# Strassen's scheme for the down products of the FFN, with sums of the hidden rows kept in DRAM

## The chip, the cores and the metric

The kernel runs on one core of a Trainium2 chip. The metric is the device time of one execution in microseconds (us); lower is better. The engines are PE (TensorE: matmuls, with its weight loads), DVE (VectorE), ACT (ScalarE), POOL (GpSimd) and SP (which issues the DMAs). Each engine works through its own instructions strictly in the order in which they were written into its queue, and waits at the first one that isn't ready.

## The reference

A step of a decoder with two layers, in fp32: 1024 prompt tokens and 64 sample tokens, width 1024. Layer 0 mixes tokens with a gated MLP, layer 1 with sliding-window attention; both have the same feed-forward network (FFN), whose hidden width is 2816:

```python
def swiglu_ffn(h, w_gate, w_up, w_down):
    return (jax.nn.silu(h @ w_gate) * (h @ w_up)) @ w_down
...
        x = x + rms_norm(out, sg_norm_post[layer] if layer < N_A_LAYERS else sw_norm_post[layer - N_A_LAYERS])
        h = rms_norm(x, f_norm_pre[layer])
        x = x + rms_norm(swiglu_ffn(h, f_w_gate[layer], f_w_up[layer], f_w_down[layer]), f_norm_post[layer])
```

The change concerns the last product, `@ w_down` (2816 to 1024 columns), in both layers.

## The kernel before

An fp32 product is made of three passes over fp32r operands. Each operand is split into a high part (ACT copies it, L275 or L510) and a low part (DVE subtracts, L276 or L511); PE then multiplies high by high, low by high and high by low. So every product costs three matmuls, and every operand one ACT copy and one DVE subtraction before PE may use it.

The hidden width is 22 feature tiles of 128, in 11 pairs. Gate and up products run pair by pair by Strassen's scheme over halves of the tokens (x: blocks 0 to 3, y: blocks 4 to 7 of 128 tokens). Each hidden tile that is finished is stored to DRAM (`store`, 256 KB each, four for a pair).

The down product comes after the last pair, in `ffn`. The 22 tiles are taken in six groups of 3, 3, 4, 4, 4 and 4. For a group, `fetch` loads the hidden tiles (all tokens, 544 KB each) and splits them, and the queue `W` delivers the split rows of `w_down`. `down(b, h, ...)` then computes block `b` (8 prompt blocks, one of samples) for one half of the columns into one PSUM bank: 3 matmuls (L1235) for each tile of the group. At its end the bank is added to the block's accumulator, a row of 1024 columns in SBUF, by DVE (L1240; ACT copies, L1238, in the first group). One block follows the other, so banks close one at a time. The next group's `fetch` is written behind the first block.

In the last group each block is finished as soon as its two banks are in (`Exit.second`): ACT squares and sums the row (L1040), DVE and POOL form the inverse root (L862, L863), DVE scales (L1042) and adds the residual row (L1043). Layer 1 then writes the result out (L1045). Layer 0 stores it (L1048), squares it again (L1049), scales it with an ACT copy (L1051), and `turn` transposes three blocks at a time on PE (L1062) for the attention of layer 1. The samples carry their two parts in two halves of 128 rows, which a small product folds (L1245, copied by L1246). The residual row of the next block is loaded while one block is finished.

The program is written in this order, but what sets the order on each engine is a scheduler that places all instructions ahead of time; on the chip the order is fixed.

Of the kernel before, what the change touches and what calls it, by code (L numbers as in the profile page):

```python
# [9 lines left out]
F32 = mybir.dt.float32  # L10
# [4 lines left out]
ALU = mybir.AluOpType  # L15
# [16 lines left out]
GROUPS = [3, 3, 4, 4, 4, 4]  # L32
HN = 512
ORDER = [0, 1, 2, 3, 8, 4, 5, 6, 7]
HD = 64
# [66 lines left out]
def trunk_kernel(ctx, tc, a):  # L102
# [317 lines left out]
    def add_ffn(layer):  # L420
        for q in range(NF):
            W.add_quad(a[("f_w_gate", "f_w_up")[q % 2]][layer], q // 2 * 2, (layer, q))
        for f in range(NF):
            W.add(a["f_w_down"][layer][f * P:(f + 1) * P, :], 1, D)
# [600 lines left out]
    class Exit:  # L1025
# [32 lines left out]
        def turn(self, c, k):  # L1058
# [5 lines left out]
            if c == 0:  # L1064
                self.x.append(act_pair())
# [15 lines left out]
    def ffn(layer, ent, last):  # L1081

        hid = [mk(dpool, [P, T], F32, f"hid{layer}_{f}") for f in range(NF)]
# [8 lines left out]
        def store(q, i, c):  # L1092
            nc.sync.dma_start(hid[q // 2 * 2 + i][:, c * HN:(c + 1) * HN], region(q, i, c))
# [11 lines left out]

        def need(name):
            flow.drain(lambda: ent.gate[name].is_open)

        def p1(q):
            need("x1")  # L1110
            if q % 2 == 0:
                rows[q // 2] = [special([P, D], "rows", bufs=2) for _ in range(2)]
# [3 lines left out]
            s["keep"] = region(q, 0, 1) if q % 2 == 0 else tmp()  # L1116
            nc.scalar.activation(s["keep"], s["a"], AF.Copy)  # L1117

        def p2(q):
            need("x2")  # L1120
            s = st[q]
            part(s["a"], unit(q, "b2"), 0, ent, "x2", False)
            r = region(q, 0, 0)
# [21 lines left out]
        def turned(q, cp):  # L1145
# [12 lines left out]
            else:  # L1158
# [3 lines left out]
                for i in range(2):  # L1162
                    nc.sync.dma_start(hid[q // 2 * 2 + i][:, SEQ:], r[:, i, :])
# [27 lines left out]
        def p3(q):  # L1191
# [4 lines left out]
            take(q, 0, 1, s["c"], s["u2"])  # L1196

# [4 lines left out]
        for fn, q in steps:  # L1202
            fn(q)
            flow.run()


        W.cap = 6
        W.prepare()
        acc = [act_tile()[:, :D] for _ in range(NB + 1)]
        parts = deque()  # L1210

        def fetch(g):
            f = sum(GROUPS[:g])
            new = []
            hs = act_tile(F32R)[:, :GROUPS[g] * P].rearrange("p (f s t) -> p f s t", s=2, t=NS)
            for i in range(GROUPS[g]):
                h, l = act_pair()
                nc.sync.dma_start(l.bitcast(F32), hid[f + i])
                split(hs[:, i, 0, :], hs[:, i, 1, :], l[:, SEQ:].bitcast(F32))
                split(h[:, :SEQ], l[:, :SEQ], l[:, :SEQ].bitcast(F32))  # L1220
                new.append((h, l))
            parts.append((new, hs.rearrange("p f s t -> p f (s t)")))

        def down(b, h, us, xs, hs, gi):
            ps = bank()
            o, n = slice(h * HN, (h + 1) * HN), len(us)
            for i, u in enumerate(us):
                wh, wl = u.hi[:, 0, o], u.lo[:, 0, o]
                if b < NB:
                    xh, xl = (t[:, b * P:(b + 1) * P] for t in xs[i])  # L1230
                    todo = [(xh, wh), (xl, wh), (xh, wl)]
                else:
                    todo = [(hs[:, i, :], wh), (hs[:, i, :], wl)]
                for j, (x, w) in enumerate(todo):
                    nc.tensor.matmul(ps, x, w, start=i == j == 0, stop=i == n - 1 and j == len(todo) - 1)  # L1235
            flow.pe(3 * n * HN / 2.4)
            if gi == 0:
                nc.scalar.activation(acc[b][:, o], ps, AF.Copy)  # L1238
            else:
                nc.vector.tensor_tensor(acc[b][:, o], ps, acc[b][:, o], op=ALU.add)  # L1240

        def folded():
            for h in range(2):
                ps = bank()
                nc.tensor.matmul(ps[:NS, :], fold, acc[NB][:, h * HN:(h + 1) * HN], start=True, stop=True)  # L1245
                nc.scalar.activation(z8[:NS, h * HN:(h + 1) * HN], ps[:NS, :], AF.Copy)  # L1246
            flow.pe(1800)
            ext.second(NB, z8)

        fetch(0)  # L1250
        for gi, gn in enumerate(GROUPS):
            xs, hs = parts.popleft()
            us = [W.get() for _ in range(gn)]
            order = list(range(NB + 1))
            final = gi == len(GROUPS) - 1
            if final:
                W.cap = 5
                ext = Exit(lambda b: ent.out[:tokens(b), b, :], ("f_norm_post", layer), last)
                order = [NB] + order[:-1] if last else order[:6] + [NB] + order[6:-1]
                ext.fetch(order[0])  # L1260
                z8 = act_tile()[:, :D]
            for j, b in enumerate(order):
                if final and j < NB:
                    ext.fetch(order[j + 1])
                for h in range(2):
                    down(b, h, us, xs, hs, gi)
                    if j == NB and h:
                        for u in us:
                            W.done(u)
                    flow.run()  # L1270
                if j == 0 and not final:
                    fetch(gi + 1)
# [404 lines left out]
```

## Time and profile before

| what | value |
|---|---|
| median of 3 runs | 2274.45 us (2274.03 to 2278.57) |
| profiled execution, its own time | 2275.59 us |
| its span | 2273.9 us |
| PE busy | 2202.6 us, 97% of the span |
| DVE busy | 1283.2 us, 56% |
| ACT busy | 810.4 us, 36% |
| DMA | 194.69 MB, mean 86 GB/s |
| down products of layer 0 | from 855.9 to about 1126.9 us |
| down products of layer 1 | from about 2004 to 2264.6 us |

The time of the profiled execution stands 1.7 us over its span. "x" in a row is a count of instructions. `PEclk` is the clock that PE was granted, 1.00 being full speed. In rows of the timeline the first two columns are the start and the length in us, and "[2.92 <-ACT act L510]" says that the engine sat idle for 2.92 us before the row, until ACT's line 510 released it. Tiles carry the names `bank` and `aux` (PSUM), `act` (SBUF operands, accumulators), `rows` and `raw` (what was loaded), `tok` (one number for a token).

### The profile page before, as it was taken

The numbers are of one execution on the slowest core, as the hardware profiler recorded it, in microseconds if no ns is written. First come the engines' busy times: TensorE is split into PE (matmuls) and PEld (weight loads), VectorE is DVE, ScalarE is ACT, GpSimd is POOL, SyncE is SP. The second block draws the span as 40 slices with busy tenths as digits, with TensorE's granted clock in tenths as the row PEclk, the third lists the DMA queues.
The fourth block names the chain that finished last, engine by engine and source line by source line (L and its number), as shares of the span: only waits on it lengthen the run. The fifth ranks groups of instructions, "written<-read, shape, count | busy, mean of one in ns | idle before, by whom it ended". The sixth has DMA issues, their size and how long they took to land.

```text
span 2273.9 us, 29115 instructions
## 1 busy us (share of the span) xinstructions
PE 2202.6 (97%) x11392; PEld 1864.3 (82%) x11392; DVE 1283.2 (56%) x2081; ACT 810.4 (36%) x1647; POOL 182.3 (8%) x222
## 2 busy tenths in 40 slices
PE   8999996999999999999999999969999999999998
PEld 7999875888888887888898877758888888878886
DVE  5465448655655653545757774477565565535446
ACT  5234424322322333211566762234232332342112
POOL 2322210000000000000213320110000000000000
PEclk9999998999999999999999998979999999999999
DMA  4211332122222234223441111221222221343224
GB/s 147 57 38 38 96 106 86 61 71 90 76 64 89 76 106 138 91 77 104 136 118 43 47 60 57 98 88 64 74 85 63 80 86 62 97 143 109 77 86 143
DMA packets 138975, 194.69 MB, mean 86 GB/s; under 512 B 22051, under 2 KB 101653, under 8 KB 138838
## 3 DMA queue, kind: packets, MB, share of 16 engines
q1 hardware_dynamic: 138838, 192.84, 26.8%
q8 instruction: 89, 1.46, 0.3%
q14 instruction: 48, 0.39, 0.1%
HBM read 143.88 MB, written 43.32 MB: 82 GB/s over the span
## 4 chain that ended last, share of the span: by engine, by line
PE 73%; DVE 5%; DMA 3%; ACT 2%; issue 1%; SPq 0%; POOL 0%; POOLq 0%; ACTq 0%; DVEq 0%
PE bank L1235 22%; PE bank L1076 11%; PE bank L1077 11%; PE bank L1078 11%; PE bank L1138 2%; PE bank L1137 2%; PE bank L873 2%; PE bank L874 1%; PE bank L505 1%; PE bank L504 1%; PE bank L506 1%; PE bank L875 1%; DVE act L276 1%; DMA act<-hid 1%; DMA raw<-in_f_w_down 1%
## 5 line engine op out<-in xcount | busy, mean ns | idle before, releaser
L1235 PE MATMUL bank<-act,act 128*128 128x512 f32 x2288 | 526.5, 392 | 5.9 <-ACT act L510 5.3
L1076 PE MATMUL bank<-act,act 128*128 128x512 f32 x1232 | 487.0, 396 | 31.0 <-ACT rows L1117 17.9
L276 DVE TENSOR_TENSOR act<-raw,act 128x1024 fp32r<-128x1024 f32 x261 | 317.5, 1223 | 352.0 <-PE bank L1077 188.3
L1235 PEld LDWEIGHTS bank<-act,act 128*128 128x128 f32 x2288 | 430.0, 189 | 100.7 <-ACT act L510 7.8
L275 ACT ACTIVATE act<-raw 128x1024 fp32r<-128x1024 f32 x261 | 275.2, 1059 | 597.7 <-PE bank L1235 203.9
L1077 PE MATMUL bank<-act,act 128*128 128x512 f32 x1232 | 485.2, 394 | 0.0
L1078 PE MATMUL bank<-act,act 128*128 128x512 f32 x1232 | 478.6, 391 | 1.2 <-DVE act L276 1.2
L1076 PEld LDWEIGHTS bank<-act,act 128*128 128x128 f32 x1232 | 232.8, 189 | 78.4 <-ACT rows L1117 18.3
L1078 PEld LDWEIGHTS bank<-act,act 128*128 128x128 f32 x1232 | 232.6, 189 | 51.0 <-DVE act L276 2.7
L1077 PEld LDWEIGHTS bank<-act,act 128*128 128x128 f32 x1232 | 233.2, 189 | 43.1
L1240 DVE TENSOR_TENSOR act<-bank,act 128x512 f32<-128x512 f32 x180 | 123.5, 688 | 150.9 <-PE bank L1235 150.7
L504 PE MATMUL bank<-act,act 128*128 128x384 f32 (+1 forms) x624 | 205.8, 332 | 2.0 <-DVE act L636 1.4
L506 PE MATMUL bank<-act,act 128*128 128x384 f32 (+1 forms) x624 | 206.8, 332 | 0.4 <-DVE act L276 0.4
L505 PE MATMUL bank<-act,act 128*128 128x384 f32 (+1 forms) x624 | 206.4, 331 | 0.0
L863 POOL TENSOR_TENSOR tok<-tok,expo 128x1 f32<-128x1 f32 (+1 forms) x63 | 54.5, 866 | 1719.3 <-DVE tok L862 1719.3
L504 PEld LDWEIGHTS bank<-act,act 128*128 128x128 f32 x624 | 117.7, 189 | 4.0 <-DVE act L636 1.6
L506 PEld LDWEIGHTS bank<-act,act 128*128 128x128 f32 x624 | 117.6, 189 | 1.9 <-issue 1.2
L505 PEld LDWEIGHTS bank<-act,act 128*128 128x128 f32 x624 | 117.8, 189 | 1.0 <-issue 0.7
L873 PE MATMUL bank<-act,act 128*128 128x512 f32 (+1 forms) x288 | 114.9, 402 | 0.6 <-DVE tok L899 0.6
L874 PE MATMUL bank<-act,act 128*128 128x512 f32 (+1 forms) x288 | 113.7, 395 | 0.0
L875 PE MATMUL bank<-act,act 128*128 128x512 f32 (+1 forms) x288 | 111.8, 393 | 0.0
L511 DVE TENSOR_TENSOR act<-act,act 128x64 fp32r<-128x64 f32 (+3 forms) x114 | 71.9, 657 | 49.9 <-ACT act L510 49.3
(231 smaller groups left out, 2628.0 us busy)
## 6 DMA issues: line engine op xcount, KB each, us to landing
act<-hid SPq DMA_DIRECT2D x44, 544.0 KB
raw<-in_f_w_gate SPq DMA_DIRECT2D x44, 512.0 KB
raw<-in_f_w_up SPq DMA_DIRECT2D x44, 512.0 KB
hid<-rows SPq DMA_DIRECT2D x88, 256.0 KB
raw<-in_f_w_down SPq DMA_DIRECT2D x44, 512.0 KB
stream<-act SPq DMA_DIRECT2D x24, 512.0 KB
rows<-stream SPq DMA_DIRECT2D x24, 512.0 KB
raw<-in_sg_w_in SPq DMA_DIRECT2D x16, 512.0 KB
```

Of the source, the lines that this page charges most:

```text
L275: nc.scalar.activation(self.hi, raw, AF.Copy)
L276: nc.vector.tensor_tensor(self.lo, raw, self.hi.bitcast(F32), op=ALU.subtract)
L504: nc.tensor.matmul(out[:, :n], h, xh[:, cs:cs + n], start=begin, stop=False)
L505: nc.tensor.matmul(out[:, :n], h, xl[:, cs:cs + n], start=False, stop=False)
L506: nc.tensor.matmul(out[:, :n], l, xh[:, cs:cs + n], start=False, stop=end)
L873: nc.tensor.matmul(ps[:m, :], xh, h, start=begins and j == 0, stop=False)
L874: nc.tensor.matmul(ps[:m, :], xl, h, start=False, stop=False)
L875: nc.tensor.matmul(ps[:m, :], xh, l, start=False, stop=ends and j == len(todo) - 1)
L1076: nc.tensor.matmul(ps, h, xh, start=begin and k == 0, stop=False, skip_group_check=not begin)
L1077: nc.tensor.matmul(ps, h, xl, start=False, stop=False, skip_group_check=not begin)
L1078: nc.tensor.matmul(ps, l, xh, start=False, stop=k == 3, skip_group_check=not begin)
L1235: nc.tensor.matmul(ps, x, w, start=i == j == 0, stop=i == n - 1 and j == len(todo) - 1)
```

## The change

The 22 tiles become 11 pairs of tiles, in two groups of 6 and 5 pairs. For a pair, write x1, x2 for the two hidden tiles of the first half of the tokens, y1, y2 for those of the second half, u1, u2 for the two tiles of `w_down` in the columns 0 to 511 and v1, v2 for those in 512 to 1023. Seven products take the place of eight. Each is a stage of its own, in this order: x1·u1, x2·u2, s3·t3, s2·t2, y2·t4, s1·t1, s4·v2, with s1 = y1 + y2, s2 = s1 − x1, s3 = x1 − y1, s4 = x2 − s2, and the t's likewise sums of u's and v's. A stage takes the pairs of its group, and for each of four blocks of 128 tokens one product of 512 columns; 14 stages in all. Below, a stage has the name of its left factor, and the two groups are called first and second.

- `sums(q)` forms s1 to s4 of a finished pair (four DVE operations of 128x512) and stores them; seven stores for a pair instead of four, into tensors with names of their own.
- In the down phase `fetch(j)` loads the left factor of a stage and its weights, two pairs in a tile of 128x1024, splits the left factor, forms t's from the weights by one DVE operation (L1271, L1273) and splits them. It runs one stage ahead. The weights no longer go through `W`. Weights come as half rows of 2 KB.
- `gather` adds a bank to every accumulator that the product belongs to: up to three DVE operations for a bank (L1318).
- The y blocks are finished in the last stage but one (s1), the x blocks in the last (s4), with 3 first in layer 0. The residual rows are two ahead.
- The attention takes its chunks of tokens in the order 2, 1, 0 (`CORDER`), and the two row tiles of a pair are taken a step later (`new_rows` in p2).

```diff
-GROUPS = [3, 3, 4, 4, 4, 4]
+PAIRS = [6, 5]
+CORDER = [2, 1, 0]
...
+        def sums(q):
+            p = q // 2
+            x1, y1, x2, y2 = (region(q, i, c) for i in range(2) for c in range(2))
+            t = act_tile()
+            s1, s2 = t[:, :HN], t[:, HN:D]
+            for n, o, u, v, op in (("s1", s1, y1, y2, ALU.add), ("s3", y1, x1, y1, ALU.subtract),
+                                   ("s2", s2, s1, x1, ALU.subtract), ("s4", x1, x2, s2, ALU.subtract)):
+                nc.vector.tensor_tensor(o, u, v, op=op)
+                nc.sync.dma_start(hid[n][:, p, :], o)
...
+        order = [("x1", "u1"), ("x2", "u2"), ("s3", "t3"), ("s2", "t2"), ("y2", "t4"), ("s1", "t1"), ("s4", "v2")]
+        stages = [(g, hn, wn) for g in range(len(PAIRS)) for hn, wn in order]
...
+                    c = chained[e]
+                    load(raw, w(second), n)
+                    if wn == "t4":
+                        nc.vector.tensor_tensor(c, raw, c, op=ALU.subtract)
+                    else:
+                        nc.vector.tensor_tensor(c, c, raw, op=ALU.add if wn == "t2" else ALU.subtract)
+                    u.split(c)
...
+        def product(ps, i, ops, begin):
+            todo = [(h, u, e) for h, u in ops for e in range(h.n)]
+            for j, (h, u, e) in enumerate(todo):
+                xh, xl = (t[:, e * HN + i * P:e * HN + (i + 1) * P] for t in (h.hi, h.lo))
+                wh, wl = (t[:, e * HN:(e + 1) * HN] for t in (u.hi, u.lo))
+                for k, (x, w) in enumerate([(xh, wh), (xl, wh), (xh, wl)]):
+                    nc.tensor.matmul(ps, x, w, start=begin and j == k == 0, stop=j == len(todo) - 1 and k == 2,
+                                     skip_group_check=not begin)
...
+            for j, (g, hn, wn) in enumerate(stages):
+                ops = fetched.popleft()
+                if j + 1 < len(stages):
+                    fetch(j + 1)
...
+                for i in [3, 0, 1, 2] if final and hn == "s4" and not last else range(4):
+                    if hn in ("x1", "s2"):
+                        banks[i] = bank()
+                    ps = aux() if hn in ("s3", "y2") else banks[i]
+                    product(ps, i, ops, hn in ("x1", "s2", "s3", "y2"))
...
+                    if final and hn in ("s1", "s4"):
+                        finish(y if hn == "s1" else x, acc[y if hn == "s1" else x])
...
+            if (fn, q) == (p2, NF - 1):
+                W.cap = 0
+                down_begin()
```

How the order moved is shown at two places. The first is on DVE in the down phase of layer 0. Before, at a change of groups (the tiles bank_8090 to bank_8189 are banks of three successive blocks, act_6994 to act_6996 their accumulators, the L511 rows the splits of the next hidden tiles):

```order
L1240 TENSOR_TENSOR act_6994<-bank_8090,act_6994 128x512
L1240 TENSOR_TENSOR act_6994<-bank_8104,act_6994 128x512
L511 TENSOR_TENSOR act_8118<-act_8120,act_8118 128x64
L511 TENSOR_TENSOR act_8120<-act_8120,act_8119 128x1024
L1240 TENSOR_TENSOR act_6995<-bank_8147,act_6995 128x512
L511 TENSOR_TENSOR act_8118<-act_8127,act_8118 128x64
L511 TENSOR_TENSOR act_8127<-act_8127,act_8126 128x1024
L1240 TENSOR_TENSOR act_6995<-bank_8161,act_6995 128x512
L511 TENSOR_TENSOR act_8118<-act_8134,act_8118 128x64
L511 TENSOR_TENSOR act_8134<-act_8134,act_8133 128x1024
L1240 TENSOR_TENSOR act_6996<-bank_8175,act_6996 128x512
```

After, where stage s2 of the second group ends and y2 begins (bank_8338 to bank_8389 are the four blocks of s2, act_8303 and act_8309 the low parts of the first left factor and the first t4 of y2):

```order
L1318 TENSOR_TENSOR act_7080<-bank_8338,act_7080 128x512
L1318 TENSOR_TENSOR act_7081<-bank_8355,act_7081 128x512
L1318 TENSOR_TENSOR act_7082<-bank_8372,act_7082 128x512
L1318 TENSOR_TENSOR act_7083<-bank_8389,act_7083 128x512
L510 TENSOR_TENSOR act_8303<-act_8303,act_8302 128x1024
L1271 TENSOR_TENSOR act_8085<-act_8307,act_8085 128x1024
L510 TENSOR_TENSOR act_8309<-act_8085,act_8308 128x1024
L510 TENSOR_TENSOR act_8315<-act_8315,act_8314 128x1024
L1271 TENSOR_TENSOR act_8099<-act_8319,act_8099 128x1024
L510 TENSOR_TENSOR act_8321<-act_8099,act_8320 128x1024
```

Before, the splits that a later block needs stand between the additions of earlier ones; after, the four additions of a stage stand ahead of all splits of the next.

The second place is on PE at the end of the down products of layer 0. Before (bank_8575 and bank_8634 are halves of two successive blocks; the L1062 rows are transposes of blocks that are finished):

```order
L1235 MATMUL bank_8575<-act_8369,act_8141 128x512
L1235 MATMUL bank_8575<-act_8370,act_8140 128x512
L1062 MATMUL aux_8589<-ident_70,act_8425 128x128
L1062 MATMUL aux_8589<-ident_70,act_8466 128x128
L1062 MATMUL aux_8597<-ident_70,act_8425 128x128
L1062 MATMUL aux_8597<-ident_70,act_8466 128x128
L1062 MATMUL aux_8605<-ident_70,act_8425 128x128
L1062 MATMUL aux_8605<-ident_70,act_8466 128x128
L1235 MATMUL bank_8634<-act_8078,act_8119 128x512
```

After (bank_8389, bank_8338, bank_8355 and bank_8372 are the blocks 3, 0, 1 and 2 of stage s4, act_8718 is the finished row of block 3):

```order
L1304 MATMUL aux_8555<-act_8551,act_7984 128x512
L1296 MATMUL bank_8389<-act_8551,act_8544 128x512
L1296 MATMUL bank_8338<-act_8551,act_8544 128x512
L1296 MATMUL bank_8355<-act_8551,act_8544 128x512
L1296 MATMUL bank_8372<-act_8550,act_8544 128x512
L1296 MATMUL bank_8372<-act_8550,act_8545 128x512
L1296 MATMUL bank_8372<-act_8551,act_8544 128x512
L1323 MATMUL aux_8732<-act_7084,fold_77 64x512
L1061 MATMUL aux_8833<-ident_70,act_8718 128x128
L1061 MATMUL aux_8833<-ident_70,act_8584 128x128
L1061 MATMUL aux_8833<-ident_70,act_8613 128x128
```

Before, transposes of finished blocks stand among the matmuls of later blocks; after, the four blocks of the stage are taken in turns and all end together, and every transpose stands behind the last down matmul.

221 lines of the change are left out of this document (142 added, 79 removed).

## The prediction

> **What bounds the kernel now.** I read the page first, then busy time by stretches of the span, then the waits of PE, and last the timeline round each wait.
>
> ```profile
> span 2273.9 us, 29115 instructions
> ...
> PE 2202.6 (97%) x11392; PEld 1864.3 (82%) x11392; DVE 1283.2 (56%) x2081; ACT 810.4 (36%) x1647; POOL 182.3 (8%) x222
> ...
> L1235 PE MATMUL bank<-act,act 128*128 128x512 f32 x2288 | 526.5, 392 | 5.9 <-ACT act L510 5.3
> ...
> L276 DVE TENSOR_TENSOR act<-raw,act 128x1024 fp32r<-128x1024 f32 x261 | 317.5, 1223 | 352.0 <-PE bank L1077 188.3
> L275 ACT ACTIVATE act<-raw 128x1024 fp32r<-128x1024 f32 x261 | 275.2, 1059 | 597.7 <-PE bank L1235 203.9
> ...
> L1240 DVE TENSOR_TENSOR act<-bank,act 128x512 f32<-128x512 f32 x180 | 123.5, 688 | 150.9 <-PE bank L1235 150.7
> ```
>
> PE is busy 97% of the time, and the 2288 down matmuls waited only 5.9 us in all. DVE and ACT have room on the mean. The stretches show where PE is full (columns: stretch, length, busy time of PE, weight loads, DVE, ACT, POOL, clock, DMA share, GB/s):
>
> ```profile
> 413.00:866.00 453.00, 448.01 (x2141) 374.65 (x2138) 262.27 (x354) 141.85 (x208) 0.00 (x0) 1.00 0.28 87
> 866.00:1124.00 258.00, 257.44 (x1130) 211.69 (x1131) 125.87 (x175) 70.83 (x107) 7.45 (x10) 0.99 0.29 99
> 1124.00:1145.00 21.00, 21.00 (x122) 20.38 (x121) 16.59 (x23) 16.26 (x28) 9.16 (x6) 1.00 0.51 163
> 2017.00:2262.00 245.00, 244.88 (x1075) 201.42 (x1076) 117.46 (x160) 54.43 (x82) 4.14 (x8) 1.00 0.28 96
> 2262.00:2274.00 12.00, 2.57 (x12) 1.79 (x10) 6.26 (x7) 1.15 (x2) 0.81 (x2) 0.78 0.34 130
> ```
>
> Inside the down phases PE has no gaps. Behind that of layer 0 (1124 to 1145) it has none either. So a matmul removed there is worth its whole interval, and every new wait there costs its whole length. What a down matmul takes:
>
> ```profile
> 2223.43 41.14 PE L1235 MATMUL bank<-act,act 128*128 128x512 f32 x180
> ```
>
> 180 matmuls take 41.14 us. Without the last one's 0.39 us and by 179 steps that is 0.2277 us for each; the 392 ns of the page are lengths that overlap.
>
> **The saving.** The prompt's down products have 2112 of the 2288 matmuls (176 are the samples'). Seven products for eight make 1848. 264 × 0.2277 = 60.1 us, 30 for each layer. The samples' 176 remain. It is the only gain of any size.
>
> **Gate and up.**
>
> ```profile
> L295 DVE TENSOR_TENSOR raw<-raw 128x512 f32<-128x512 f32 x14 | 9.6, 687 | 0.2
> ```
>
> This addition of the gate and up phase has the size of those in `sums`: four for a pair are 2.8 us, with three more stores. DVE is busy 262 of 453 us there, so the idle 191 us hide 11 × 2.8 = 31 us, and I cost it at nothing; without that cover it would be these 31 us for a layer. The later `new_rows` may let ACT's first write of a pair wait for a store of the pair before; PE has the products of the other half of the tokens meanwhile, and ACT is busy 142 of 453 us: nothing. `CORDER` exchanges the order of chunks: nothing.
>
> **The start of the down phase.**
>
> ```profile
> 850.00:860.00 10.00, 8.76 (x38) 6.40 (x37) 6.51 (x12) 3.91 (x7) 0.00 (x0) 1.00 0.79 273
> 860.00:866.00 6.00, 3.64 (x15) 2.48 (x15) 1.25 (x2) 0.70 (x2) 0.00 (x0) 0.98 0.99 337
> 866.00:880.00 14.00, 13.44 (x47) 10.85 (x48) 5.22 (x7) 8.12 (x15) 0.00 (x0) 0.76 0.27 109
> 2000.00:2010.00 10.00, 8.62 (x35) 5.93 (x34) 5.32 (x9) 2.41 (x4) 0.00 (x0) 1.00 0.91 306
> 2010.00:2020.00 10.00, 9.72 (x43) 7.56 (x42) 4.25 (x7) 7.65 (x14) 0.00 (x0) 1.00 0.33 132
> ```
>
> Before, the DMA engines are full here (share 0.99) and PE loses 1.2 + 2.4 + 0.6 us and a clock of 0.76 for 14 us (3.4), then 1.4 + 0.3 in layer 1: 9.3 in all. After, x1 of the first group needs only pairs stored long ago and is loaded under the last gate and up products. But x2's 3.1 MB come while the last rows are stored and SP still issues x1's loads. Both ends are open: no wait at all gives −9, twice the old loss +9. I take nearly the old loss, 8, since the same queue moves about the same bytes: net −1.
> Later, a stage with two weight tensors to combine loads 4.7 MB in 16.4 to 19.1 us (72 matmuls, 12 more with samples), 247 to 288 GB/s. The row at share 0.99 moved 337, so it fits: nothing.
>
> **The boundaries between stages.** PE takes the four blocks of a stage in turns in the second group, so their banks close together, and DVE's order has the additions of a stage ahead of the first splits of the next. PE's first matmul then waits for a chain. Prices: addition 0.69 (L1240), split or t 1.22 (L276, the same size), high copy 1.06 (L275). In each layer:
> - y2, first group: two additions, split, t4, copy: 4.9 us.
> - x2, second group: thirteen additions and two splits, 11.4 us from the first closed bank, against 23 matmuls of its own meanwhile (5.2): 6.2.
> - s3 to s2: six additions, split, t2, copy 7.6, against 17 matmuls (3.9): 3.7.
> - y2, second group: four additions, split, t4, copy 6.3, less the last three matmuls (0.7): 5.6.
> - s1: addition, t1, copy 3.0, and 0.4 earlier for a bank: 3.4.
> - s4: four additions and two splits 5.2, against 12 matmuls (2.7): 2.5.
>
> That is 26 us for a layer, 52 in both. The low end is what hangs on a bank closed by the very last matmul (y2 twice, s1): 27. The high end takes the row of the one such hand-over before:
>
> ```profile
> PE bank L1076 <- DVE tmp L1181: 2.7, 2, 1.4
> ```
>
> There one addition of 0.69 made PE wait 1.4: 0.7 more at each of 12 places, 60.
>
> **The clock after a wait.**
>
> ```profile
> 866.56 3.78 PE L1235 MATMUL bank<-act,act 128*128 128x512 f32 x8 [2.92 <-ACT act L510]
> ...
> 376.30 0.79 PE L1076 MATMUL bank<-act,act 128*128 128x512 f32 x1 [4.86 <-ACT act L275]
> ```
>
> ```profile
> 376.00:378.00 2.00, 1.70 (x6) 1.52 (x7) 2.00 (x3) 0.82 (x3) 0.00 (x0) 0.50 0.60 165
> 378.00:380.00 2.00, 2.00 (x11) 2.00 (x11) 1.33 (x4) 0.00 (x0) 0.55 (x1) 0.50 0.74 251
> 380.00:382.00 2.00, 2.00 (x11) 1.81 (x10) 0.65 (x2) 1.47 (x3) 0.06 (x1) 0.73 0.32 133
> 382.00:384.00 2.00, 2.00 (x13) 1.74 (x12) 1.47 (x2) 1.10 (x2) 0.49 (x1) 1.00 0.31 129
> ```
>
> After 4.86 us of idling PE runs at 0.50 for about 4.8 us and loses 2.4. The 2.92 us of 866, after other waits, had eight matmuls in 3.78 us, half speed too. Waits of 4.5 us and more without a break are the two y2 of each layer and the end of layer 0: 5 × 2.4 = 12 us. Low end 5 (two), high end 26 (eleven).
> The Trainium skill has a rule for this ("TensorE: Matmul & The Clock Gate", section "What's actually happening"): after about 3.4 us without work the clock is halved, and some 3.4 us of sustained work bring it back. By the rule the term would be an estimated 5 × 1.7 = 8.5 us, the sum 3.5 lower; the trace took 4.8 us to come back, and it decides.
>
> **The end of layer 0.** What finishing a block costs:
>
> ```profile
> L1042 DVE SCALAR_TENSOR_TENSOR act<-act,tok,act 128x1024 f32<-128x1024 f32 x7 | 9.0, 1279 | 1.0 <-POOL tok L863 0.7
> L1043 DVE TENSOR_TENSOR act<-act,rows 128x1024 f32<-128x1024 f32 x7 | 8.5, 1220 | 0.0
> L1040 ACT ACTIVATE act<-act 128x1024 f32<-128x1024 f32 x7 | 7.4, 1055 | 10.6 <-DVE act L1240 10.6
> L1051 ACT ACTIVATE act<-act,tok 128x1024 f32<-128x1024 f32 x6 | 6.9, 1151 | 10.6 <-POOL tok L863 10.6
> ...
> L1040 ACT ACTIVATION_READ_ACCUMULATOR act<-act 128x1 f32 x7 | 1.3, 187 | 0.0
> ...
> L1246 ACT ACTIVATE act<-bank 64x512 f32<-64x512 f32 x2 | 1.1, 583 | 0.0
> ```
>
> The first transpose is of block 3, which ACT finishes only after 11 squares (1.06 + 0.19), 6 scaled copies (1.15) and the two fold copies (0.58) that stand ahead of it behind the last matmul: 13.7 + 6.9 + 1.2 = 21.8 us, with a first addition and hand-overs 23. DVE has about as much (five additions, five scalings, six residual additions and smaller ones). Before, PE had no gap here. Then transposes go at DVE's pace: 2 more, 25. Low end 18 (three squares of y blocks done earlier), high end 32 (each residual row waits for the row buffer that an addition two blocks back frees).
>
> **The end of layer 1.**
>
> ```profile
> 2264.95 0.68 DVE L1240 TENSOR_TENSOR act<-bank,act 128x512 f32<-128x512 f32 x1
> 2265.06 5.58 SPq L1045 DMA_DIRECT2D out_y_prompt<-act  x2
> ...
> 2269.05 1.23 DVE L1043 TENSOR_TENSOR act<-act,rows 128x1024 f32<-128x1024 f32 x1
> ```
>
> Before, one block is left: from the last matmul (2264.6) to the end 9.3 us, 3.6 of them after the last addition. After, DVE has five additions, and scalings and residual additions of four x blocks, the samples and two y blocks left: 3.5 + 7 × (1.28 + 1.22) = 21.0, and 3.6 to the end: 24.6, so 15 more. Low end 11 (no y block left), high end 21 (rows late).
>
> **Sum.** −60.1 − 1 + 52 + 12 + 25 + 15 = +43 on the profiled execution's 2275.6: 2318.5. That execution lies 1.1 over the median of the runs: 2317. All low ends together give −60.1 − 9 + 27 + 5 + 18 + 11 = −8, 2266; all high ends −60.1 + 9 + 60 + 26 + 32 + 21 = +88, 2362; not all fall on one side.
>
> **Rivals.**
> - Faster. PE's waits at the boundaries stay as small as before. For it speaks that the down matmuls waited 5.9 us before with the same prices, and that DVE is at 56%: it may be through with a stage's operands a stage ahead. Against it, the splits stand behind the additions in DVE's queue, so its idle time can't be used. If boundaries and clock cost 6 us, the sum is −60.1 − 1 + 6 + 25 + 15 = −15: 2259. It decides where the twelve boundaries and the clock cost together less than 21 us, 1.75 each.
> - No change: half of these waits are covered by loads and splits that run earlier, and 21 us remain: 2274.
> - Slower still: the loads are late. If DMA gives the 273 GB/s of 850 to 860 with its waits, and 200 on the mean under stores, 4.7 MB take 23.5 us against 17.7: 5.8 us in each of eight stages with t3 or t1, 46 more: 2363. Against it: 337 GB/s at share 0.99, and loads run a stage ahead.
>
> **How the numbers follow.** The forecast has 0.71, faster 0.16, no change 0.05, loads late 0.08. What a measurement can tell from no change is about 0.2%, 4.5 us. So slower 0.79, same 0.05, faster 0.16. The forecast's own range is 2282 to 2352; to leave out no more than 2 in 10 the range goes down to the upper part of the faster case: 2263 to 2352.
>
> **What would show it.** Right: 1848 prompt matmuls; PE waits of 4 to 6 us for ACT's high copies at y2, several us for DVE at x2, s2, s1 and s4; clock rows of 0.5 behind them; an idle PE of 20 us or more behind the down matmuls of layer 0; some 25 us from the last matmul to the end. Wrong: PE at 97% inside the down phase, or transposes that start within 10 us of the last down matmul.

## The result and the profile after

The changed kernel takes 2341.76 us (median of 4 runs, 2340.36 to 2343.31), the kernel before 2274.24 on the same chip: a ratio of 1.0295 (95% interval 1.0277 to 1.0313), 67 us slower. The forecast was 2317 in a range of 2263 to 2352: the direction and the range hold, the size is 25 us short. The profiled execution has 2341.45 us, 0.3 below the median.

The head of the page and its costliest groups (busy time, mean ns, idle time ahead of them and its releaser):

```profile
span 2339.7 us, 29144 instructions
PE 2167.6 (93%) x11128; PEld 1829.3 (78%) x11128; DVE 1430.6 (61%) x2209; ACT 863.7 (37%) x1675; POOL 188.6 (8%) x222
...
L1296 PE MATMUL bank<-act,act 128*128 128x512 f32 x1320 | 327.3, 403 | 34.5 <-ACT act L1316 18.8
...
L1296 PE MATMUL aux<-act,act 128*128 128x512 f32 x528 | 131.4, 409 | 23.3 <-ACT act L509 20.5
```

1320 + 528 are the 1848 prompt matmuls of the forecast. PE has 264 matmuls fewer but is busy only 35 us less than before (2202.6), where 264 × 0.2277 are 60: part of what runs, runs at a lower clock. And the down products, which waited 5.9 us in all before, now have 34.5 + 23.3 us of idle time ahead of them. PE's waits by what it waited for (total, times, longest):

```profile
PE aux L1061 <- ACT act L1050: 23.3, 1, 23.3
PE aux L1296 <- ACT act L509: 20.5, 4, 5.3
PE bank L1296 <- ACT act L1316: 18.8, 2, 10.5
```

The two down phases (882 to 1133 and 2060 to 2309) and what lies behind each, in the columns of the prediction's stretches:

```profile
882.00:1133.00 251.00, 228.13 (x932) 181.00 (x932) 148.28 (x171) 78.62 (x94) 3.98 (x4) 0.94 0.48 159
1133.00:1156.00 23.00, 0.00 (x0) 0.00 (x0) 18.52 (x30) 18.78 (x30) 14.51 (x12) 0.54 0.75 249
1156.00:1186.00 30.00, 27.99 (x150) 24.24 (x151) 15.81 (x26) 16.18 (x31) 2.62 (x4) 0.78 0.28 94
2060.00:2309.00 249.00, 225.87 (x929) 181.00 (x930) 146.25 (x168) 75.63 (x91) 3.99 (x4) 0.95 0.48 161
2309.00:2339.00 30.00, 1.49 (x5) 0.26 (x3) 19.49 (x24) 6.38 (x12) 4.23 (x5) 0.56 0.66 228
```

932 matmuls at 0.2277 are 212.2 us, but PE is busy 228.1: 15.9 us more in layer 0, and by the same reckoning 14.3 in layer 1. Most of this is the clock: busy time times (1 − PEclk), added up over stretches of 0.5 us, gives 12.4 us in layer 0 and 11.6 in layer 1. The rest is chiefly the last matmuls ahead of waits, which show their whole 0.39 us, and the four matmuls of the fold (2.9 us). Behind layer 0 PE stands still for 23 us while ACT and DVE are busy some 18.5 each. The timeline of PE in layer 0's down phase shows the waits one by one:

```profile
882.50 5.91 PE L1296 MATMUL bank<-act,act 128*128 128x512 f32 x18 [10.52 <-ACT act L1316]
940.95 17.94 PE L1296 MATMUL aux<-act,act 128*128 128x512 f32 x72 [4.95 <-ACT act L509]
...
1052.84 15.48 PE L1296 MATMUL bank<-act,act 128*128 128x512 f32 x60 [2.07 <-ACT act L509]
1073.63 12.01 PE L1296 MATMUL aux<-act,act 128*128 128x512 f32 x45 [5.31 <-ACT act L509]
...
1092.76 0.50 PE L1304 MATMUL aux<-act,act 128*128 128x512 f32 x1 [3.05 <-ACT act L509]
1113.65 0.50 PE L1296 MATMUL bank<-act,act 128*128 128x512 f32 x1 [1.67 <-DVE act L1318]
```

They stand where the forecast put them: y2 of the first group (941, forecast 4.9), x2 of the second (1013 to 1020, 3.3 in four pieces, forecast 6.2), s3 to s2 (1053, with 0.93 ahead of it 3.0, forecast 3.7), y2 of the second (1074, with 0.33 more 5.6, forecast 5.6), s1 (1093, 3.05, forecast 3.4) and s4 (1114, with 0.63 more 2.3, forecast 2.5). The first row, 10.52, is another thing: the start.

### The profile page after: what moved, and what is told of

Same layout as the page of the kernel before. It is cut to its first block, busy times and chain, and to the rows that moved or that the text cites. A ratio compares the mean times of both kernels' runs of the same rounds, so it can differ in the third digit from the quotient of the medians.

```text
span 2339.7 us, 29144 instructions
## 1 busy us (share of the span) xinstructions
PE 2167.6 (93%) x11128; PEld 1829.3 (78%) x11128; DVE 1430.6 (61%) x2209; ACT 863.7 (37%) x1675; POOL 188.6 (8%) x222
## 4 chain that ended last, share of the span: by engine, by line
PE 72%; DVE 7%; ACT 2%; issue 2%; DMA 2%; POOL 1%; SPq 0%; DVEq 0%; ACTq 0%; POOLq 0%
PE bank L1296 13%; PE bank L1075 12%; PE bank L1076 12%; PE bank L1077 12%; PE aux L1296 5%; PE bank L503 2%; PE bank L1158 2%; PE bank L1157 2%; PE bank L504 2%; PE bank L505 2%; PE aux L1304 2%; PE bank L872 1%; PE bank L873 1%; PE bank L874 1%; DVE act L1318 1%
## 5 line engine op out<-in xcount | busy, mean ns | idle before, releaser
L1075 PE MATMUL bank<-act,act 128*128 128x512 f32 x1232 | 486.8, 396 | 28.6 <-ACT rows L1135 18.0
L1076 PE MATMUL bank<-act,act 128*128 128x512 f32 x1232 | 485.0, 394 | 0.0
L1077 PE MATMUL bank<-act,act 128*128 128x512 f32 x1232 | 475.3, 391 | 1.2 <-DVE act L277 1.2
L277 DVE TENSOR_TENSOR act<-raw,act 128x1024 fp32r<-128x1024 f32 x217 | 265.4, 1228 | 239.3 <-ACT act L276 73.7
L1296 PE MATMUL bank<-act,act 128*128 128x512 f32 x1320 | 327.3, 403 | 34.5 <-ACT act L1316 18.8
L276 ACT ACTIVATE act<-raw 128x1024 fp32r<-128x1024 f32 x217 | 226.8, 1058 | 309.3 <-DVE raw L297 190.2
L1296 PEld LDWEIGHTS bank<-act,act 128*128 128x128 f32 x1320 | 256.0, 195 | 95.3 <-ACT act L1316 19.6
L509 ACT ACTIVATE act<-act 128x1024 fp32r<-128x1024 f32 (+5 forms) x194 | 167.5, 905 | 337.7 <-DVE act L1273 93.9
L1075 PEld LDWEIGHTS bank<-act,act 128*128 128x128 f32 x1232 | 232.9, 189 | 75.5 <-ACT rows L1135 18.3
L1077 PEld LDWEIGHTS bank<-act,act 128*128 128x128 f32 x1232 | 232.5, 189 | 51.1 <-DVE act L277 2.7
L1076 PEld LDWEIGHTS bank<-act,act 128*128 128x128 f32 x1232 | 233.3, 189 | 43.1
L510 DVE TENSOR_TENSOR act<-act,act 128x1024 fp32r<-128x1024 f32 (+5 forms) x194 | 194.2, 1036 | 99.4 <-ACT act L509 99.2
L862 POOL TENSOR_TENSOR tok<-tok,expo 128x1 f32<-128x1 f32 (+1 forms) x63 | 60.7, 970 | 1738.6 <-DVE tok L861 1738.6
L1296 PE MATMUL aux<-act,act 128*128 128x512 f32 x528 | 131.4, 409 | 23.3 <-ACT act L509 20.5
L1296 PEld LDWEIGHTS aux<-act,act 128*128 128x128 f32 x528 | 104.0, 199 | 49.7 <-ACT act L509 23.3
L503 PEld LDWEIGHTS bank<-act,act 128*128 128x128 f32 x624 | 117.8, 189 | 4.6 <-DVE act L635 1.6
L504 PEld LDWEIGHTS bank<-act,act 128*128 128x128 f32 x624 | 118.2, 190 | 1.0 <-issue 0.9
L505 PEld LDWEIGHTS bank<-act,act 128*128 128x128 f32 x624 | 118.1, 189 | 1.0 <-DVE act L277 0.7
L872 PE MATMUL bank<-act,act 128*128 128x512 f32 (+1 forms) x288 | 113.9, 399 | 1.0 <-DVE tok L898 0.6
```

The costliest lines, as they stand in the source:

```text
L276: nc.scalar.activation(self.hi, raw, AF.Copy)
L277: nc.vector.tensor_tensor(self.lo, raw, self.hi.bitcast(F32), op=ALU.subtract)
L503: nc.tensor.matmul(out[:, :n], h, xh[:, cs:cs + n], start=begin, stop=False)
L504: nc.tensor.matmul(out[:, :n], h, xl[:, cs:cs + n], start=False, stop=False)
L505: nc.tensor.matmul(out[:, :n], l, xh[:, cs:cs + n], start=False, stop=end)
L509: nc.scalar.activation(hi, src, AF.Copy)
```

## The start: a queue that waits, and a queue behind it

SP's queue and the stretches of it in layer 0, then ACT's rows ahead of PE's 10.52:

```profile
849.63 0.32 SPq L1097 DMA_DIRECT2D hid_y<-rows  x1
856.96 0.32 SPq L1097 DMA_DIRECT2D hid_x<-rows  x1
```

```profile
852.00:858.00 6.00, 6.00 (x29) 4.90 (x29) 2.03 (x5) 0.28 (x1) 0.00 (x0) 1.00 0.03 13
...
864.00:870.00 6.00, 6.00 (x29) 4.95 (x27) 1.23 (x1) 1.06 (x1) 0.00 (x0) 1.00 0.96 348
...
876.00:882.00 6.00, 0.00 (x0) 0.00 (x0) 4.55 (x4) 4.21 (x7) 0.00 (x0) 0.50 1.04 402
```

```profile
875.04 1.06 ACT L509 ACTIVATE act<-act 128x1024 fp32r<-128x1024 f32 x1 [3.97 <-DMA act<-hid_x]
...
881.86 2.05 ACT L1316 ACTIVATE act<-bank 128x512 f32<-128x512 f32 x4
```

SP stands at a store of the last pair (L1097) from 850 to 857, because the row to be stored isn't ready. x2's loads are behind it, and the DMA engines move 13 GB/s. Then they run full, at 348 to 402 GB/s. ACT takes x2's splits (L509) as they land; the copies of x1's closed banks (L1316) stand behind them in ACT's queue, and PE needs those banks for x2. The last of these banks closes at 872.0, but the copies run at 881.9, and PE stands 10.5 us, in layer 1 8.3.

## The experiments

Each is compared with the kernel before on its own chip; the medians of the kernel before on these chips lie between 2272.7 and 2274.2 us. A trace is of one execution, up to 7 us off the median of its kernel.

**order_all: PE takes the blocks of a stage one after the other.**

```diff
+            return end.ins
...
+                turn = None
...
-                    product(ps, i, ops, hn in ("x1", "s2", "s3", "y2"))
+                    with tc.issue_after(turn) if turn and (True) else nullcontext():
+                        turn = product(ps, i, ops, hn in ("x1", "s2", "s3", "y2"))
```

> Only PE's order is changed: in each stage the four blocks are taken one after the other, not in turns. Theory A (queue order: blocks that end together put a stage's additions ahead of the next stage's splits in DVE's queue): PE's waits inside the down phases, 22 us in each layer without the start, fall below 8 us, and the slow clock behind them goes with them; the time falls from 2342 by 30 to 50 us, to 2292 to 2312. The 23 us at the end of layer 0 stay, since its rows and squares still come late. Theory B (bytes and work: the added loads and DVE operations are what PE waits for, in whatever order): the waits move but their sum stays above 35 us, and the time is within 12 us of 2342.

2313.69 us, ratio 1.0180 (1.0164 to 1.0195), 28 less than the changed kernel. Its waits:

```profile
PE aux L1061 <- ACT act L1050: 18.0, 1, 18.0
...
PE aux L1296 <- ACT act L509: 15.9, 11, 2.8
```

Behind the start no wait inside a phase is over 2.8 us, but they add up to 13 us in layer 0 and 14.5 in layer 1 (from 22 each), not to less than 8: the time misses theory A's range by 2 us, and theory B's by more. The waits of the second group fall by 22 us in both layers together, those of the first grow by 5. Layer 0's end costs 18.0 instead of 23.3, which I had not expected; that it is because the banks of y close one by one is likely, but not shown. The turns are a cost of this change, but not the only one: 40 us over the kernel before remain.

**rows_deep: five residual rows ahead, in tiles of `act`, in place of two in the row buffer.**

```diff
-                if ahead and len(e.r) < 2:
+                while ahead and len(e.r) < 5:
```

> Up to five residual rows are loaded ahead for the finishing, in tiles of their own, instead of two. If the ends are long because each residual row waits for a buffer, the three row loads in the last chain (4.2, 4.0 and 5.5 us) go and the end of layer 1 shrinks from 30 to 20 us or less, that of layer 0 from 23 to 20: 10 to 15 us faster than 2342. If ACT's and DVE's own work sets the ends (21 us each), the time falls by less than 5 us.

2343.81 us, ratio 1.0313 (1.0296 to 1.0329): no gain. The traced execution took 2348.28, 4.5 over the median. In it the two ends go opposite ways. The wait behind layer 0 grew:

```profile
1167.25 2.18 PE L1063 MATMUL aux<-ident,act 128*128 128x128 f32 x9 [29.53 <-ACT act L1052]
```

There the finishing also stands in another order: DVE adds five residual rows in one go, and ACT waits twice for POOL:

```profile
1152.83 2.41 ACT L1052 ACTIVATE act<-act,tok 128x1024 f32<-128x1024 f32 x2 [4.63 <-POOL tok L862]
1159.82 1.15 ACT L1052 ACTIVATE act<-act,tok 128x1024 f32<-128x1024 f32 x1 [4.58 <-POOL tok L862]
```

At the end of layer 1 the loads of rows, which the chain of work of the changed kernel names three times, left that chain, and from the last product to the end it takes 25.3 us instead of 30.2. The longest of the three before:

```profile
2329.15 5.48 DMA rows<-stream
```

So late rows do hold the end of layer 1, for 5 us; the longer wait behind layer 0 takes the gain away.

**order_rows: both.**

The edits are those of order_all and of rows_deep.

> Both: blocks one after the other on PE, and five residual rows ahead. Theory A: the blocks are finished while later blocks are multiplied, so the idle time behind layer 0's down products falls from 23 to about 10 us and the end of layer 1 from 30 to about 12; with the waits inside gone too the time is 2265 to 2290. Theory B: the ends shrink by what the rows alone bring, the inside stays: 2325 to 2340.

2306.39 us, ratio 1.0150 (1.0131 to 1.0168). This lies in neither range. The end of layer 0 still costs 19.6 us (theory A had 10); that of layer 1 takes 18.2 us from the last product, where order_all has 25.2. So the row loads are worth some 7 us, at the end of layer 1, once the banks close one by one.

**act_first: the last splits of x2 behind the copies of x1's banks, on ACT.**

```diff
+                    with tc.issue_after(copied[0]):
+                        fetch(1, 1, rest)
```

> The last splits of stage x2 in the first group are put behind ACT's five copies of stage x1's banks. If the waits at the start (10.5 and 8.3 us) come from these copies standing in ACT's queue behind splits that wait for their loads, each falls below 3 us and the time falls by 12 to 20 us. If the loads of x2 themselves are late, PE waits for them instead, and the time is within 4 us of 2342.

2336.95 us, ratio 1.0282 (1.0267 to 1.0298), 5 less than the changed kernel, but not clear of the noise: the intervals of the two ratios overlap, and the traced execution took 2341.48. What follows is read from the trace alone. The wait for ACT's copies fell from 18.8 to 11.9 us:

```profile
PE bank L1298 <- ACT act L1319: 11.9, 2, 6.5
```

In layer 0 the copies now run at 878.5, 3.3 us earlier. They can't run sooner, because the splits that still stand ahead of them wait for their loads:

```profile
875.78 1.06 ACT L509 ACTIVATE act<-act 128x1024 fp32r<-128x1024 f32 x1 [3.37 <-DMA act<-hid_x]
...
878.54 2.05 ACT L1319 ACTIVATE act<-bank 128x512 f32<-128x512 f32 x4
```

The order on ACT is half a reason: behind it the data are late.

**early1: x2's loads are written ahead of the last pair's stores.**

```diff
-                if j + 1 < len(stages):
+                if j and j + 1 < len(stages):
...
+            if (fn, q) == (p657, NF - 1):
+                fetch(1)
```

> The loads of stage x2 of the first group are written before the last pair's sums, so that SP issues them ahead of the last four stores of hidden rows. Theory A for the start: SP's queue. In the changed kernel SP stands 7 us at a store that waits for DVE, the DMA engines move nothing from 852 to 858 us, and x2's loads stand behind; ahead of them, the two waits of 10.5 and 8.3 us fall below 4 us each, with the half clock behind them, and the time falls by 12 to 25 us from 2342. Theory B: the DMA engines are full (400 GB/s at 876 to 882 us), the bytes come no sooner, and the time stays within 5 us.

2321.24 us, ratio 1.0223 (1.0194 to 1.0251), 20.5 less. Both waits at the start are gone, and SP's dead stretch carries loads now:

```profile
852.00:858.00 6.00, 6.00 (x29) 4.95 (x28) 3.34 (x7) 2.17 (x3) 0.00 (x0) 1.00 0.54 171
```

The other waits stay as they were (4.92 and 5.31 at y2, 23.22 behind layer 0). In the traces the gain is 18.8 us of waits and some 3 us of clock. So the start is shown: SP's queue first, ACT's queue behind it.

**half_loads: t3 and t1 with one weight tensor loaded instead of two.** The kernel leaves out the first tensor's load; the subtraction takes the second twice, so its results are not the reference's, and 512 KB less come for each two pairs.

```diff
-                        load(chained[e], w(first), n)
...
+                    if first:
+                        nc.vector.tensor_tensor(c, raw, raw, op=ALU.subtract)
```

> In the stages s3 and s1 the first of two weight tensors isn't loaded; t3 and t1 are formed by one DVE operation of the same size from the other alone (so these weights are left out, and the results are not the reference's). 24 loads of 512 KB fewer, the same work on PE, DVE and ACT. Theory B (bytes): waits inside the down phases fall by a third or more, 10 to 20 us faster than 2342. Theory A (queue order): the waits at y2, x2, s2 and s1 stay as they are, and the time is within 5 us of 2342.

2333.07 us, ratio 1.0267 (1.0250 to 1.0283), 9 less. The boundaries hardly answer:

```profile
1071.13 12.71 PE L1297 MATMUL aux<-act,act 128*128 128x512 f32 x45 [4.18 <-ACT act L509]
```

y2 of the first group keeps 4.87, that of the second goes from 5.31 to 4.18, s1 from 3.05 to 0.92. In the other layer it is the same, which makes 7 of the 9 us. The gain lies between the two expectations: loads being late is a small part, and the rival that had them cost 46 us falls.

**filler: 92 matmuls without use behind layer 0's last fold, so that the clock is full when the transposes come.**

```diff
+                with tc.issue_after(folds[-1]):
+                    junk = bank()
+                    h, u = ops[-1]
+                    for k in range(92):
+                        nc.tensor.matmul(junk, h.hi[:, :P], u.hi[:, :HN], start=k == 0, stop=k == 92 - 1)
```

> 92 matmuls without a use (21 us of PE time) stand behind the down products of layer 0, ahead of the transposes; nothing else is moved. If the clock sets the pace behind the 23 us of idling (0.78 from 1156 to 1186 us), PE now comes out of it at full clock and the time falls by 3 to 7 us from 2342. If ACT's and DVE's turns set the pace there, or the added matmuls end too late, the time is the same or up to 3 us longer.

2346.29 us, ratio 1.0324 (1.0305 to 1.0343): no gain. PE is busy for 25.5 of the 26 us from 1130 to 1156, and the clock behind it rises from 0.78 to 0.94:

```profile
1156.00:1186.00 30.00, 25.54 (x157) 22.80 (x158) 16.73 (x29) 17.35 (x33) 2.08 (x5) 0.94 0.35 114
```

In that stretch PE does about the same work with 2.5 us less busy time, and nothing comes earlier. The first transposes still wait 2.1 us for ACT. There the pace is that of ACT and DVE; the clock costs nothing at this place.

**order_early: order_all and early1.**

The edits are those of order_all and of early1.

> Blocks one after the other on PE, and x2's loads ahead of the last stores. If the two are separate causes their gains add: 28 us from the order and what early1 gives, 2285 to 2303. If one wait hides the other, the time is no more than 5 us below the 2314 of the order alone.

2302.85 us, ratio 1.0134 (1.0115 to 1.0152). The gains do not add: 28 and 20.5 apart give 39 together. With both, no wait inside the phases is over 2.9 us, but they still add up to 16 us in each layer. The ends are 22 us (layer 0) and 16 us (layer 1) longer than before, and 30 us over the kernel before remain.

**oe_56: order_early with the groups exchanged, so that s1 and s4 of the last group are longer.**

```diff
-PAIRS = [6, 5]
+PAIRS = [5, 6]
```

> order_early with the groups exchanged (5 pairs first, 6 last), so that the last stages s1 and s4 of a layer have 72 matmuls instead of 60, 2.7 us more each by 0.2277. Theory (the ends are set by the finishing of four blocks on ACT and DVE inside these two stages): ACT and DVE get 5.5 us more ahead of the last matmul, the idle time behind layer 0's down products falls from 18.2 us to about 13, the end of layer 1 by as much: 2303 - 10 = 2293, 2290 to 2297. Rival (the first squares wait for tiles that only the last matmuls of s1 and the last splits free, and all the finishing follows from there): the longer s1 gives nothing, only the longer s4 does: 2.7 for each end, 2297 to 2300. Second rival (the finishing behind the last matmul alone counts): 18.2 stays, 2303.

2303.64 us, ratio 1.0135 (1.0115 to 1.0154): no gain in the median. But three runs took 2302 to 2306 us and the traced one 2296.78. In that one the wait behind layer 0 is 16.2, 2 less than in order_early, and from the last product to the end it takes 18.4 us, where order_early has 25.3:

```profile
1132.11 2.18 PE L1061 MATMUL aux<-ident,act 128*128 128x128 f32 x9 [16.23 <-ACT act L1050]
```

So the medians speak against the theory that ACT and DVE only lack time in the last two stages, and the one trace speaks for it: this stays open. Another lack is suggested by the rows of ACT: its first square of a y block comes at 1111.9 in the changed kernel, only 21 us ahead of the end of PE's last product, and at 1093.6 in order_early, 22 us ahead.

```profile
1111.90 1.06 ACT L1039 ACTIVATE act<-act 128x1024 f32<-128x1024 f32 x1 [5.18 <-DVE act L1318]
```

```profile
1093.56 1.06 ACT L1039 ACTIVATE act<-act 128x1024 f32<-128x1024 f32 x1 [1.96 <-DVE act L510]
```

No y block can be finished before its s1 bank and no x block before its s4 bank, however long these stages are. That this order sets the tail is argued from the trace, not shown; the next runs test the ends from the other side, with another order of the work.

**hyb54: nine pairs by Strassen ([5, 4]), the last four tiles as one plain group, finished block by block as before; with the edits of order_early and chunks 0, 1, 2.**

```diff
-PAIRS = [6, 5]
+PAIRS = [5, 4]
+GROUPS = [4]
...
+            for gi, gn in enumerate(GROUPS):
...
+                    if final and b < NB:
+                        ext[0].second(b, acc[b])
```

> Strassen's scheme for the first nine pairs only (groups of 5 and 4, blocks one after the other on PE, x2's loads ahead of the last stores); the last two pairs as one plain group of four tiles with the finishing of the kernel before, nine blocks one after the other in 48 us. 216 matmuls fewer than the kernel before, 49 us. If the long ends come from finishing eight blocks in two stages, both ends return to the lengths before (383 us from the last down product of layer 0 to the first gate product of layer 1, 9.3 us at the end), and only the boundaries (some 20 us a layer with the clock) are left: 2273 - 49 + 40 - 9 at the start = 2255, 2245 to 2270. If the ends are long because of the stage's work itself (ACT and DVE behind by then), they stay at 410 and 25: above 2285.

2286.97 us, ratio 1.0057 (1.0040 to 1.0073). The 23 us behind layer 0 are gone (no wait over 2.8 us there): from its last product to the first gate product of layer 1 it takes 393 us, and 10.7 us at the end of layer 1, near the 383 and 9.3 of before. But the total is 17 us above the range that I expected, and by the number alone it is the rival's. The waits inside the phases stay, many and short: 21 us in layer 0 and 18 in layer 1, beside some 12 us of clock.

```profile
PE aux L1319 <- ACT act L513: 12.0, 11, 2.3
```

**hyb6: six pairs by Strassen in one group of seven stages, the other ten tiles in plain groups of 3, 3 and 4.**

```diff
-PAIRS = [6, 5]
+PAIRS = [6]
+GROUPS = [3, 3, 4]
```

> The same with Strassen's scheme for the first six pairs in one group of seven stages, and the last ten tiles in plain groups of 3, 3 and 4. 144 matmuls fewer, 33 us. Half the stages, so half the boundaries (10 us a layer): 2273 - 33 + 20 - 9 = 2251, 2243 to 2268. If boundaries cost little here and matmuls are all that counts, it is slower than the nine-pair version by the 16 us of matmuls.

2264.81 us (6 runs), ratio 0.9962 (0.9948 to 0.9975): faster than the kernel before by 0.4%, and 77 us faster than the changed one. With one group, which is also the first, each bank is added once instead of up to three times, and few waits are left:

```profile
PE aux L1319 <- ACT act L513: 8.6, 4, 2.9
```

It has 144 matmuls fewer than the kernel before, worth 32.8 us, of which 9 arrive.

**hyb6_turns: hyb6 with the blocks of a stage in turns, as in the change.**

```diff
-                    with tc.issue_after(turn) if turn and (True) else nullcontext():
-                        turn = product(ps, i, ops, hn in ("x1", "s2", "s3", "y2"))
+                    product(ps, i, ops, hn in ("x1", "s2", "s3", "y2"))
```

> hyb6 (six pairs by Strassen, the other ten tiles in plain groups with the finishing of before) but with the four blocks of a stage in turns on PE as in the change. Theory (turns make the four banks of a stage close together, so that the next stage waits for their additions): the second group of the change had 3.3 + 2.1 + 5.3 + 3.0 + 1.7 = 15 us of waits for a layer against about 3 x 2.9 in hyb6: 4 to 7 us more for a layer, 2273 to 2279, and the gain over the kernel before is gone. Rival (the turns only cost where a layer's end hangs on them, and the plain groups catch up): 2262 to 2268.

2269.18 us (10 runs), ratio 0.9986 (0.9976 to 0.9995): 4 us more than hyb6, between the two expectations, and the intervals of the two ratios do not overlap. The one wait of 4.87 at y2 is back,

```profile
932.84 18.21 PE L1319 MATMUL aux<-act,act 128*128 128x512 f32 x72 [4.87 <-ACT act L513]
```

in place of several shorter ones in hyb6. New are waits where the plain groups begin, 3.4 us in layer 0 and 3.6 in layer 1, of which hyb6 has none:

```profile
990.74 0.50 PE L1425 MATMUL bank<-act,act 128*128 128x512 f32 x1 [0.70 <-DVE act L1341]
...
996.44 96.56 PE L1425 MATMUL bank<-act,act 128*128 128x512 f32 x417 [1.90 <-ACT act L513]
```

All waits of the down phases together are 22 us here and 16 in hyb6; the two traced executions took about the same (2267.15 and 2268.01), so it is the medians that tell the kernels apart. In one group, then, the turns cost little; most of the 28 us that order_all took out belong to the second group, whose waits fell by 22 us there, and to the ends that hang on it, which this kernel doesn't have.

## Why the prediction was right in direction and short in size

The terms, in us, against what the trace of the changed kernel has:

| term | predicted | measured | from |
|---|---|---|---|
| matmuls | −60 | −60 | 1848 in place of 2112, by 0.2277 |
| gate and up | 0 | 0 | below |
| start | −1 | +9 | 18.8 of waits, less the 9.3 of before |
| boundaries | +52 | +45 | 22.2 in layer 0, 22.7 in layer 1 |
| clock | +12 | +24 | 12.4 and 11.6 inside the two phases |
| end of layer 0 | +25 | +25 | below |
| end of layer 1 | +15 | +21 | last product to end 30.2, 9.3 before |
| sum | +43 | +64 | spans: +65.8 |

The measured terms come from different views; the 2 us between their sum and the spans are not assigned.

*Matmuls, gate and up.* As predicted. The same stretch of 450 us of layer 1's gate and up phase, before and after:

```profile
1530.00:1980.00 450.00, 448.43 (x2176) 376.23 (x2177) 267.09 (x367) 144.47 (x217) 0.00 (x0) 1.00 0.23 72
```

```profile
1565.00:2015.00 450.00, 448.42 (x2177) 376.29 (x2177) 294.45 (x407) 146.34 (x218) 0.00 (x0) 1.00 0.29 91
```

DVE has 27 us more (the estimate was 31), and PE does not notice.

*Start: the failed step.* "I take nearly the old loss, since the same queue moves about the same bytes" looked at bytes. What counts is the place in the queue: x2's loads stand behind a store that waits, and the copies of x1's banks behind splits that wait for x2. The high end, +9, is what came in waits alone; early1 took 20.5 us out with what hangs on them.

*Boundaries: the mechanism and the size are right.* Ten single waits were forecast within 1 us of what came. Only x2 of the second group is half as long (3.3 for 6.2), since PE takes single matmuls between the additions, some of them at half clock. At s2 and s1 PE waits for ACT's copy, the last link of the chain that was priced, and not for DVE, as the signs had it. The rival that had these waits stay small is refuted.

*Clock: the mis-sized term.* I counted waits of 4.5 us and more, five. The clock fell behind shorter ones too:

```profile
1052.80:1054.80 2.00, 1.96 (x5) 1.58 (x6) 2.00 (x3) 0.93 (x1) 0.00 (x0) 0.55 0.98 360
1054.80:1056.80 2.00, 2.00 (x6) 1.54 (x6) 1.52 (x2) 0.39 (x1) 0.00 (x0) 0.59 0.88 343
1056.80:1058.80 2.00, 2.00 (x10) 1.66 (x9) 1.30 (x2) 1.19 (x2) 0.00 (x0) 1.00 0.57 159
...
1092.80:1094.80 2.00, 2.00 (x7) 1.67 (x8) 2.00 (x2) 0.86 (x1) 0.00 (x0) 0.80 1.01 390
1094.80:1096.80 2.00, 2.00 (x5) 0.63 (x4) 1.44 (x2) 0.48 (x1) 0.00 (x0) 0.50 1.01 401
```

A wait of 2.07 us and one of 3.05 us are followed by a clock of 0.5 for 3 to 4 us. But not every wait is: in layer 1 the clock stays at 1.00 behind 3.14 us at s1, and behind 2.42 us at s4.

```profile
2273.32 0.50 PE L1304 MATMUL aux<-act,act 128*128 128x512 f32 x1 [3.14 <-ACT act L509]
```

```profile
2272.00:2274.00 2.00, 0.68 (x3) 0.60 (x4) 0.74 (x2) 1.79 (x2) 0.00 (x0) 1.00 0.98 380
2274.00:2276.00 2.00, 2.00 (x9) 1.20 (x8) 2.00 (x3) 0.22 (x1) 0.00 (x0) 1.00 1.03 412
```

The clock fell at all seven stops of layer 0 and at five of the seven of layer 1. These twelve falls cost 24 us, 2.0 each; a single one lasts about 3.4 us and costs 1.4 to 1.7. So the price of 2.4 was somewhat high and the count far too low: my high end, eleven waits or 26 us, was the better count. The Trainium skill ("TensorE: Matmul & The Clock Gate", section "What's actually happening") puts the fall of the clock behind about 3.4 us without work; the row of 2.07 us disagrees, and the measurement decides. Its 3.4 us of work for the return fits the first of these waits (work again at 1052.8, full clock from about 1056.4). At the end of layer 0, which I had among the five, filler showed that the clock costs nothing.

*End of layer 0.* PE's wait is 23.3 us, where 23 were worked out. ACT does just what was listed, 11 squares, six scaled copies and the two fold copies, so the mechanism is right. That the size fits so well is in part luck: the work takes some 19 us instead of 21.8, and the 4.2 us that ACT waits for POOL in between were not in the working.

```profile
1147.35 1.15 ACT L1050 ACTIVATE act<-act,tok 128x1024 f32<-128x1024 f32 x1 [2.81 <-POOL tok L862]
1150.87 1.15 ACT L1050 ACTIVATE act<-act,tok 128x1024 f32<-128x1024 f32 x1 [1.34 <-POOL tok L862]
```

From the last product (1132.9) to the first product of layer 1's gate and up phase the changed kernel takes 412.3 us, the kernel before 383.3 (from 1126.9):

```profile
1545.25 0.79 PE L1075 MATMUL bank<-act,act 128*128 128x512 f32 x1 [9.27 <-ACT rows L1135]
```

```profile
1510.16 0.80 PE L1076 MATMUL bank<-act,act 128*128 128x512 f32 x1 [9.19 <-ACT rows L1117]
```

Of these 29 us 3.6 are 24 transposes that PE did ahead of that mark before, and has behind it now: 25 are left, as predicted.

*End of layer 1.* 21 for 15, the high end, whose reason was given as rows that come late. The runs bear this out: the chain names the rows, and with the rows loaded earlier (rows_deep) the end takes 25.3 us, where 24.6 were worked out without late rows.

*The ends as a cause.* With order_early they still cost 18 us of waiting in layer 0 and 25 from the last product in layer 1; longer last stages gave nothing in the median, and with the finishing spread over a plain group (hyb54, hyb6) the ends were within 10 us (layer 0) and 1.4 us (layer 1) of the old ones. What holds the four x blocks inside the tail of order_early was not isolated.

## What to carry to other kernels

Fewer matmuls are worth their time only where the chain that hands the banks on is as loose as before: price each boundary by the additions, the subtraction and the copy behind the last closed bank, and add some 2 us of half clock for most waits of 2 us and more. Before loads are moved, read what they stand behind in SP's queue, and what stands behind their consumers in ACT's: a store that waits holds every load behind it. And a saving of this kind may be had in part: one group by the scheme, the rest in the old way, kept the old end and was the only version that beat the kernel before.

## What the runs showed of the hardware

The clock of PE fell to 0.5 behind a wait of only 2.07 us in one place, and stayed at 1.00 behind 3.14 us in another. DMA moved 402 GB/s at a share of 1.04 (876 to 882), where I had taken the 337 GB/s of a share of 0.99 for its limit. And in the middle of a phase that is short of loads, the DMA engines moved 13 GB/s for 6 us, since one store in SP's queue waited.
